# A decoder layer's FFN in three passes: the first pass's down products as seven block products too, an earlier start for the next pass's sums, and other places for the norms' transposes

## Chip, cores and metric

The kernel runs on one core of a Trainium2 chip. The metric is the device time of one execution in microseconds (us), as the median of several runs. TensorE (PE) multiplies, VectorE (DVE) and ScalarE (ACT) work elementwise, GpSimd (POOL) raises a few small tiles to a power, and SyncE (SP) issues the transfers.

## What is computed

One layer of a hybrid decoder on 2048 prompt tokens and 32 sample tokens, in float32 (D = 1024, hidden size 2816, per-layer input of 256):

```
h = h + concat(gated recurrence, conv module) @ w_out        # the mix phase
xn2 = rmsnorm(h, norm_ffn)
h = h + (silu(xn2 @ w_ffn_gate) * (xn2 @ w_ffn_up)) @ w_ffn_down
gate = sigmoid(rmsnorm(h, norm_ple) @ w_ple_gate)
h = h + gate * (p_l @ w_ple_proj)
y = rmsnorm(h, norm_final)
```

## The kernel before

**Arithmetic.** Each float32 operand is split into a high and a low part: ACT copies the rounded high part (L385), DVE subtracts it for the low part (L390, or L393 as a scalar_tensor_tensor where a gain is multiplied in). A product is then three matmuls (high x low, high x high, low x high), which stand in the profile as L542 to L544 for a plain product and as L1627 for one of seven block products. A tile's high part ends in h (wh, xh, x2h, xoh, hxh), its low part in l.

**Phases.** The mix phase goes over 8 blocks of 256 tokens and ends near 960 us. Then the FFN, the per-layer input and the final norm run in three passes t = 0, 1, 2, each over two halves h of 348, 348 and 344 tokens. The hidden size is cut into six chunks of 4, 4, 4, 4, 2 and 4 times 128 (CHUNKS). A pass consists of these stages:

- z, gate and up products (gate_up, L1647): four block products of weights and inputs done as seven by Strassen's sums. The inputs' sums X2[kp] (named A12, A11, S1, S2, S4, S3, A22 for each of four kp) are made by combine(t, kp) (L1371), which norm2(t) starts;
- d, down products of one chunk. In pass 0 they are plain (down, L1827): 8 x 2 x nk products into the residual res, nk the chunk's size. In passes 1 and 2 the chunks of size 4 are made as seven block products for each of four row pairs q (down_sevens, L1750); split_down (L1559) makes the weights' differences, hidden_sums (L1738) the sums of hidden tiles, add_part (L1812) adds each product to the residual. The chunk of size 2 is plain in every pass;
- pin, the per-layer inputs' splits (pin_load, L1969), then p, the embedding stage (embed, L1858): for each of 8 output tiles 16 gate products and 4 projections. norm3 (L1947) splits the residual with its gain for it (h2_split, L1927) and computes the scale row r3; norm4 (L1952) is the final norm with 16 STTs (scalar_tensor_tensor, L393 h<-h,gn,px) and the stores of y.

d of chunks 0 to 3 stands behind the first z of the chunk after; d of chunk 4, d of chunk 5 and p follow one another at the end of a pass.

**A norm's chain** (rms2, L1287): squares and their sums on DVE, a memset (L1310), three transposes of the sums on PE (L1315), two reductions on DVE (L1319, L1322), a power on POOL (L426), three transposes on PE that broadcast the result over all partitions (L1330), and a copy on ACT or the STTs of norm4.

**What sets the order.** The program is written by a list scheduler in Python, Sched (L94). Every piece of work is a generator that asks for buffers of a pool, waits for events and issues instructions. Sched keeps a clock of its own for each engine and records, at every step, the instruction that could start first by these clocks. The order of the records is each engine's order on the chip. An instruction for PE from a side thread (all but lane and ffn) that isn't ready at PE's clock is put back by the number SIDE. The numbers have no meaning on the chip except through the order. Weights come over one DMA queue on SP, into a ring of NRING = 9 pairs of split tiles.

Which chunks take the seven-product form is decided by

```python
def in_sevens(t, c):
    return t in SEVENS and CHUNKS[c] == 4
```

## Time and profile before

| | |
|---|---|
| median of 3 runs | 2650.96 us (2650.74 to 2653.5) |
| profiled execution | 2655.51 us, span 2653.8 us |
| PE busy | 2527.6 us, 95% |
| DVE busy | 1964.1 us, 74% |
| ACT busy | 1070.1 us, 40% |
| mean granted clock of PE | 0.976 |

The span runs from the first to the last instruction in the trace; 1.7 us of the profiled execution lie outside it. "Busy" is the union of an engine's instructions. Matmuls overlap in the trace: one of 348 columns is shown with 0.32 us while the next starts 0.16 us after it, so their spacing is read from starts. The granted clock is 1.00 at TensorE's 2.4 GHz and lower where it ran at 1.2 GHz for part of a stretch.

### The profile page before, as it was taken

What the parts mean: (1) busy time and instruction counts of PE and PEld (TensorE: products, weight loads), DVE (VectorE), ACT (ScalarE), POOL (GpSimd) and SP (SyncE); (2) the same over time, 40 slices, a digit from 0 to 9 for tenths busy, and PEclk for the clock granted to TensorE, in tenths of its full rate; (3) what the DMA queues carried; (4) which work ended last, traced back from release to release, by engine and by line L of the source; (5) the groups of instructions that cost most, each with busy time, mean ns of one, the idle gap of its engine ahead of it and who ended that gap; (6) DMA issues with size and microseconds to landing.
All of it is one profiled execution on the core that took longest, in us unless ns stands there. A gap on an engine that the chain in (4) does not pass through costs nothing.

```text
span 2653.8 us, 44060 instructions
## 1 busy us (share of the span) xinstructions
PE 2527.6 (95%) x15646; PEld 2369.5 (89%) x15646; DVE 1964.1 (74%) x4558; ACT 1070.1 (40%) x2457; POOL 137.9 (5%) x286
## 2 busy tenths in 40 slices
PE   7999999999999799999999799999989799999986
PEld 6987977778888699999999799999989799999976
DVE  8998899678886776676677856786587676667765
ACT  5553344333332343444344343344344233333341
POOL 0111010010110100000000000000000000000000
PEclk9999999999999799999999899999999899999998
DMA  8665745655447674565452475454623645554321
GB/s 312 221 212 186 238 159 191 208 168 168 155 147 207 213 261 155 195 213 179 157 200 72 139 243 182 159 165 168 235 63 104 195 156 191 195 199 164 119 75 51
DMA packets 287630, 465.62 MB, mean 175 GB/s; under 512 B 46256, under 2 KB 87728, under 8 KB 287408
## 3 DMA queue, kind: packets, MB, share of 16 engines
q1 hardware_dynamic: 287408, 462.79, 52.3%
q8 instruction: 123, 2.02, 0.3%
q14 instruction: 99, 0.81, 0.1%
HBM read 363.03 MB, written 99.64 MB: 174 GB/s over the span
## 4 chain that ended last, share of the span: by engine, by line
PE 87%; DVE 6%; DMA 3%; ACT 1%; POOL 1%; issue 1%; SPq 0%; DVEq 0%; ACTq 0%; POOLq 0%
PE pm L1627 27%; PE px L1627 13%; PE pm L542 11%; PE pm L544 11%; PE pm L543 11%; PE px L544 2%; PE px L542 2%; PE px L543 2%; DVE h L390 1%; DVE h L393 1%; PE pm L610 1%; PE pm L612 1%; PE pm L611 1%; DMA wl<-wcl 1%; DVE wl L390 1%; POOL sm L426 1%
## 5 line engine op out<-in xcount | busy, mean ns | idle before, releaser
L390 DVE TENSOR_TENSOR wl<-raw,wh 128x512 fp32r<-128x512 f32 (+1 forms) x476 | 315.2, 666 | 171.4 <-ACT wh L385 167.7
L385 ACT ACTIVATE wh<-raw 128x512 fp32r<-128x512 f32 (+1 forms) x476 | 283.9, 608 | 326.0 <-PE pm L543 112.8
L542 PE MATMUL pm<-xal,wh 128*128 128x256 f32 (+2 forms) x960 | 323.6, 337 | 8.6 <-DVE xal L390 4.5
L544 PE MATMUL pm<-xah,wl 128*128 128x256 f32 (+2 forms) x960 | 310.6, 324 | 1.0 <-DMA wl<-wcl 0.7
L543 PE MATMUL pm<-xah,wh 128*128 128x256 f32 (+2 forms) x960 | 310.4, 323 | 0.0
L542 PE MATMUL pm<-xol,wh 128*128 128x348 f32 (+4 forms) x762 | 254.4, 334 | 6.2 <-DVE h L390 3.6
L544 PE MATMUL pm<-xoh,wl 128*128 128x348 f32 (+4 forms) x762 | 250.0, 328 | 0.6 <-DVE wl L390 0.3
L543 PE MATMUL pm<-xoh,wh 128*128 128x348 f32 (+4 forms) x762 | 249.8, 328 | 0.0
L390 DVE TENSOR_TENSOR h<-pm,h 128x348 f32<-128x348 f32 (+1 forms) x335 | 172.3, 516 | 88.7 <-PE pm L544 42.4
L1627 PE MATMUL pm<-xal,wh 128*128 128x348 f32 (+1 forms) x707 | 228.6, 323 | 3.7 <-DVE f L390 1.8
L1627 PE MATMUL pm<-xah,wh 128*128 128x348 f32 (+1 forms) x707 | 227.8, 322 | 0.0
L1627 PE MATMUL pm<-xah,wl 128*128 128x348 f32 (+1 forms) x707 | 227.5, 322 | 0.1
L542 PEld LDWEIGHTS pm<-xal,wh 128*128 128x128 f32 x960 | 182.8, 190 | 35.7 <-issue 9.2
L393 DVE SCALAR_TENSOR_TENSOR t<-u,cvw,t 128x256 f32<-128x256 f32 x448 | 212.6, 475 | 0.0
L544 PEld LDWEIGHTS pm<-xah,wl 128*128 128x128 f32 x960 | 182.0, 190 | 15.8 <-DMA wl<-wcl 1.8
L543 PEld LDWEIGHTS pm<-xah,wh 128*128 128x128 f32 x960 | 182.7, 190 | 11.7
L385 ACT ACTIVATE wh<-tw 128x512 fp32r<-128x512 f32 x146 | 91.9, 630 | 249.8 <-DVE tw L390 92.9
L1627 PE MATMUL pm<-x2l,wh 128*128 128x348 f32 (+1 forms) x533 | 171.5, 322 | 6.1 <-DVE x2l L390 6.1
L393 DVE SCALAR_TENSOR_TENSOR h<-u,cvw,h 128x256 f32<-128x256 f32 x360 | 170.2, 474 | 2.2 <-ACT h L385 2.1
L1627 PE MATMUL pm<-x2h,wh 128*128 128x348 f32 (+1 forms) x533 | 171.8, 322 | 0.0
L1627 PE MATMUL pm<-x2h,wl 128*128 128x348 f32 (+1 forms) x533 | 171.6, 322 | 0.0
L426 POOL TENSOR_TENSOR sm<-sm,mhalf 128x2 f32<-128x2 f32 (+3 forms) x79 | 72.7, 922 | 1853.9 <-DVE sm L1322 1739.2
(292 smaller groups left out, 6498.4 us busy)
## 6 DMA issues: line engine op xcount, KB each, us to landing
raw<-w_gu SPq DMA_DIRECT2D x220, 256.0 KB, 3.1
wh<-wch SPq DMA_DIRECT2D x192, 256.0 KB, 2.7
wl<-wcl SPq DMA_DIRECT2D x192, 256.0 KB, 3.1
wh<-tch SPq DMA_DIRECT2D x176, 256.0 KB, 4.3
wl<-tcl SPq DMA_DIRECT2D x176, 256.0 KB, 4.6
raw<-w_dn SPq DMA_DIRECT2D x132, 256.0 KB, 3.3
tch<-wh SPq DMA_DIRECT2D x88, 256.0 KB, 2.8
tcl<-wl SPq DMA_DIRECT2D x88, 256.0 KB, 2.9
```

The lines of the kernel that those rows point to most:

```text
L385: nc.scalar.activation(out, in_, func, scale=scale, bias=bias, **kw)
L390: return op("dve", d_tt(n), lambda: nc.vector.tensor_tensor(out=out, in0=a, in1=b, op=o), R, W)
L393: return op("dve", d_tt(n, not isinstance(s, float)), lambda: nc.vector.scalar_tensor_tensor(out=out, in0=a, scalar=s, in1=b, op0=o0, op1= ...
L426: return op("pool", 700.0, lambda: nc.gpsimd.tensor_tensor(out=s.ap[0:rows, out:out + n], in0=s.ap[0:rows, lo:lo + n], in1=mhalf[0:rows, 0 ...
L542: nc.tensor.matmul(out, lhsT=wh, rhs=xl, start=first, stop=False)
L543: nc.tensor.matmul(out, lhsT=wh, rhs=xh, start=False, stop=False)
L544: nc.tensor.matmul(out, lhsT=wl, rhs=xh, start=False, stop=last)
L610: nc.tensor.matmul(bank.ap, lhsT=xs[0], rhs=wl, start=(k == 0), stop=False)
L611: nc.tensor.matmul(bank.ap, lhsT=xs[0], rhs=wh, start=False, stop=False)
L612: nc.tensor.matmul(bank.ap, lhsT=xs[1], rhs=wh, start=False, stop=(k == KD - 1))
L1627: nc.tensor.matmul(out, lhsT=a, rhs=b, start=first and i == 0, stop=last and i == 2, skip_group_check=True)
```

## The change

Three edits. SEVENS takes in pass 0, so its five chunks of size 4 are made as seven block products. SIDE becomes a table by thread name: 4000 for norm, norm_ahead, norm2, norm3 and norm4, 2000 for layer_norm, 1000 for the rest. And norm2(t) for t > 0, before it starts the sums of pass t, no longer waits for the scale rows r3 of pass t - 1; it still waits for the last hidden tiles and for the per-layer inputs' splits.

```diff
-SEVENS = (1, 2)
+SEVENS = (0, 1, 2)
@@
-    SIDE = 1000.0
+    SIDE = dict(norm=4000.0, norm_ahead=4000.0, layer_norm=2000.0, norm2=4000.0, norm3=4000.0, norm4=4000.0)
@@
-                    s += self.SIDE
+                    s += self.SIDE.get(th[0].__name__, 1000.0)
@@
             for k in range(2):
                 for h in HALVES:
                     yield wait(("pin", t - 1, k, h))
-            for h in HALVES:
-                yield wait(("r3", t - 1, h))
```

Two lines fall away, so that lines behind norm2 have numbers lower by two in the changed kernel (L1627 is L1625 there).

What the planner makes of it is seen in the order. First PE at the start of pass 0's embedding stage, from the transposes of the first half's sums (L1315) to the broadcast of their power (L1330). Before:

```order
L544 MATMUL pm_175<-xoh,wl_87 128x348
L1315 MATMUL px_179<-idn,h_77 128x128 x2
L1315 MATMUL px_179<-idn,h_77 92x128
L542 MATMUL pm_175<-xol,wh_86 128x348
L543 MATMUL pm_175<-xoh,wh_86 128x348
L544 MATMUL pm_175<-xoh,wl_87 128x348
...
L542 MATMUL px_181<-hxl,wh_86 128x348
L543 MATMUL px_181<-hxh,wh_86 128x348
L544 MATMUL px_181<-hxh,wl_87 128x348
L1330 MATMUL px_182<-idn,sm_66 128x128 x2
L1330 MATMUL px_182<-idn,sm_66 128x92
```

The dots leave out 12 matmuls. After:

```order
L544 MATMUL px_182<-hxh,wl_87 128x348
L1315 MATMUL px_180<-idn,h_77 128x128 x2
L1315 MATMUL px_180<-idn,h_77 92x128
L542 MATMUL px_182<-xol,wh_86 128x348
L543 MATMUL px_182<-xoh,wh_86 128x348
L544 MATMUL px_182<-xoh,wl_87 128x348
L1330 MATMUL px_179<-idn,sm_66 128x128 x2
L1330 MATMUL px_179<-idn,sm_66 128x92
L542 MATMUL px_182<-hxl,wh_88 128x348
```

Between transposes and broadcast stood 18 matmuls, and now 3.

DVE at the same place: the reductions of the sums (L1319, L1322), then the STT splits of the residual (xol, hxl). Before:

```order
L1319 TENSOR_REDUCE sm_66<-px_179 128x2
L393 SCALAR_TENSOR_TENSOR xol<-h_78,gn,xoh 128x348
L1322 TENSOR_REDUCE sm_66<-px_179 92x1
L393 SCALAR_TENSOR_TENSOR xol<-h_79,gn,xoh 128x348
L393 SCALAR_TENSOR_TENSOR xol<-h_78,gn,xoh 128x348 x2
L390 TENSOR_TENSOR h_78<-pm_177,h_78 128x348
```

After (wl_95, wl_83 and wl_85 are the low parts of the per-layer inputs):

```order
L1319 TENSOR_REDUCE sm_66<-px_180 128x2
L393 SCALAR_TENSOR_TENSOR xol<-h_78,gn,xoh 128x348
L1322 TENSOR_REDUCE sm_66<-px_180 92x1
L393 SCALAR_TENSOR_TENSOR xol<-h_78,gn,xoh 128x348
L393 SCALAR_TENSOR_TENSOR xol<-h_76,gn,xoh 128x348
L393 SCALAR_TENSOR_TENSOR hxl<-h_76,gn,hxh 128x348
L393 SCALAR_TENSOR_TENSOR xol<-h_79,gn,xoh 128x348 x3
L393 SCALAR_TENSOR_TENSOR xol<-h_78,gn,xoh 128x348 x2
L390 TENSOR_TENSOR wl_95<-f_9124,wh_94 128x348
L390 TENSOR_TENSOR wl_83<-h_77,wh_82 128x348
L390 TENSOR_TENSOR wl_85<-h_77,wh_84 128x348
L390 TENSOR_TENSOR h_78<-pm_175,h_78 128x348
```

Behind the second reduction stood 3 STTs before the next addition from PSUM (pm), and now 8 STTs and three splits.

DVE at the head of pass 1, where norm4's 16 STTs of pass 0 (h<-h,gn,px) meet the splits of pass 1's sums (x2l). Before:

```order
L1322 TENSOR_REDUCE sm_71<-px_182 92x1
L393 SCALAR_TENSOR_TENSOR f_9124<-f_9124,gn,r_116 128x348
L393 SCALAR_TENSOR_TENSOR h_77<-h_77,gn,r_116 128x348
...
L393 SCALAR_TENSOR_TENSOR h_76<-h_76,gn,px_179 128x348 x3
L393 SCALAR_TENSOR_TENSOR h_79<-h_79,gn,px_179 128x348 x2
L393 SCALAR_TENSOR_TENSOR h_78<-h_78,gn,px_179 128x348 x3
L393 SCALAR_TENSOR_TENSOR h_76<-h_76,gn,px_182 128x348 x2
L393 SCALAR_TENSOR_TENSOR h_79<-h_79,gn,px_182 128x348 x3
L393 SCALAR_TENSOR_TENSOR h_78<-h_78,gn,px_182 128x348 x3
L390 TENSOR_TENSOR x2l<-f_9127,x2h 128x348
```

After:

```order
L393 SCALAR_TENSOR_TENSOR h_76<-h_76,gn,px_180 128x348 x3
L390 TENSOR_TENSOR wl_87<-raw_103,wh_86 128x512
L393 SCALAR_TENSOR_TENSOR h_79<-h_79,gn,px_180 128x348 x2
L393 SCALAR_TENSOR_TENSOR h_78<-h_78,gn,px_180 128x348 x3
L1322 TENSOR_REDUCE sm_69<-px_179 92x1
...
L390 TENSOR_TENSOR x2l<-f_9125,x2h 128x348
...
L393 SCALAR_TENSOR_TENSOR h_76<-h_76,gn,px_180 128x348 x2
L393 SCALAR_TENSOR_TENSOR h_79<-h_79,gn,px_180 128x348 x3
L393 SCALAR_TENSOR_TENSOR h_78<-h_78,gn,px_180 128x348 x3
L390 TENSOR_TENSOR x2l<-f_9126,x2h 128x348
```

The 16 STTs stood in one row ahead of a split; now they stand in two rows of 8, each behind other splits of sums.

## Rows read from the trace of the kernel before

**Rows 1.** The page's head, its first part (busy time of each engine) and the shares by engine of the chain that ended last.

```profile
span 2653.8 us, 44060 instructions
PE 2527.6 (95%) x15646; PEld 2369.5 (89%) x15646; DVE 1964.1 (74%) x4558; ACT 1070.1 (40%) x2457; POOL 137.9 (5%) x286
PE 87%; DVE 6%; DMA 3%; ACT 1%; POOL 1%; issue 1%; SPq 0%; DVEq 0%; ACTq 0%; POOLq 0%
```

**Rows 2.** What PE waited for over the whole span: the line that waited, the line it waited for, us in total, times, the longest.

```profile
PE px L1330 <- POOL sm L426: 21.3, 9, 5.6
PE px L1315 <- DVE sm L1310: 10.9, 5, 4.5
PE px L1627 <- DVE x2l L390: 9.5, 1, 9.5
```

**Rows 3.** The span in windows: pass 0's z and d stages, pass 0's embedding stage, the head of pass 1, pass 1's embedding stage. Columns: length, busy time (and instructions) of each engine, granted clock of PE, share of the DMA engines, GB/s.

```profile
core 0: us, PE busy (x) PEld busy (x) DVE busy (x) ACT busy (x) POOL busy (x), PEclk, DMA share, GB/s
960.40:1428.60 468.20, 465.14 (x2918) 463.37 (x2917) 320.27 (x574) 205.60 (x395) 2.52 (x2) 1.00 0.53 183
1428.60:1507.00 78.40, 77.88 (x495) 77.53 (x494) 64.37 (x136) 37.28 (x78) 3.27 (x2) 1.00 0.30 97
1507.00:1539.00 32.00, 17.54 (x85) 16.16 (x85) 23.73 (x52) 8.33 (x18) 1.67 (x2) 0.68 0.76 224
1981.00:2072.00 91.00, 82.33 (x497) 80.68 (x498) 72.64 (x154) 44.15 (x93) 6.33 (x2) 0.94 0.31 98
```

**Rows 4.** Timeline of PE at the end of pass 0's embedding stage: the first and the last of 34 matmuls of 348 columns that start one after the other. Columns: start, duration, engine, line, tile.

```profile
1501.75 0.32 PE L542 MATMUL pm<-hxl,wh 128*128 128x348 f32 x1
...
1506.99 0.32 PE L1627 MATMUL px<-xal,wh 128*128 128x348 f32 x1
```

**Rows 5.** Down stages as windows, columns as in rows 3: the first and the last chunk of pass 0 (plain), chunks 0, 1 and 2 of pass 1 (seven products), the last chunk of pass 1 and of pass 2 (seven products).

```profile
1026.10:1058.70 32.60, 32.60 (x204) 32.60 (x205) 17.67 (x31) 5.91 (x10) 0.00 (x0) 1.00 0.32 114
1398.10:1428.60 30.50, 30.50 (x194) 30.50 (x193) 21.96 (x44) 15.84 (x33) 0.00 (x0) 1.00 0.18 56
1592.50:1621.40 28.90, 28.63 (x177) 27.73 (x176) 25.59 (x56) 8.48 (x17) 0.00 (x0) 1.00 0.17 58
1673.90:1702.70 28.80, 28.53 (x175) 27.62 (x175) 25.50 (x56) 8.42 (x17) 0.00 (x0) 1.00 0.17 56
1756.00:1785.40 29.40, 29.01 (x183) 28.23 (x182) 27.95 (x64) 11.63 (x24) 0.85 (x1) 1.00 0.32 105
1951.50:1981.00 29.50, 27.27 (x164) 25.57 (x162) 27.70 (x62) 13.28 (x29) 0.00 (x0) 1.00 0.23 73
2509.40:2538.60 29.20, 26.91 (x165) 25.22 (x163) 27.43 (x62) 13.15 (x29) 0.00 (x0) 1.00 0.23 69
```

**Rows 6.** DVE's instructions by form in pass 1 (1560 to 1950): splits of weights, weight differences and a hidden tile's split (sums and additions of 348 columns take as long). Columns: instructions, busy us, mean ns of one, idle time before them and what ended it.

```profile
L390 DVE TENSOR_TENSOR wl<-tw,wh 128x512 fp32r<-128x512 f32 x35 | 24.2, 691 | 8.2 <-ACT wh L385 7.5
L390 DVE TENSOR_TENSOR tw<-raw,tw 128x256 f32<-128x256 f32 x34 | 14.2, 418 | 0.2
L390 DVE TENSOR_TENSOR xol<-h,xoh 128x348 fp32r<-128x348 f32 x27 | 13.6, 516 | 3.0 <-ACT xoh L385 3.0
L390 DVE TENSOR_TENSOR wl<-raw,wh 128x256 fp32r<-128x256 f32 x17 | 7.1, 415 | 0.0
```

**Rows 7.** Timelines at the start of pass 1's embedding stage: PE from the sums' transposes to where the spacing of matmuls returns to 0.16 us (in brackets idle time before and what ended it), then DVE, then POOL.

```profile
1983.13 0.55 PE L1315 MATMUL px<-idn,h 128*128 128x128 f32 x3
1990.76 0.84 PE L1330 MATMUL px<-idn,sm 128*128 128x128 f32 x3 [5.64 <-POOL sm L426]
1994.20 0.66 PE L542 MATMUL pm<-xol,wh 128*128 128x348 f32 x1 [2.60 <-ACT wh L385]
...
1999.93 0.34 PE L544 MATMUL pm<-xoh,wl 128*128 128x348 f32 x1
...
1985.01 1.55 DVE L393 SCALAR_TENSOR_TENSOR xol<-h,gn,xoh 128x348 fp32r<-128x348 f32 x3
...
1989.43 0.57 DVE L393 SCALAR_TENSOR_TENSOR hxl<-h,gn,hxh 128x348 fp32r<-128x348 f32 x1
...
1985.23 5.48 POOL L426 TENSOR_TENSOR sm<-sm,mhalf 128x3 f32<-128x3 f32 x1 [192.58 <-DVE sm L1322]
```

**Rows 8.** The same at the start of pass 0's embedding stage: PE, DVE, POOL.

```profile
1430.09 0.49 PE L1315 MATMUL px<-idn,h 128*128 128x128 f32 x3
1433.96 0.51 PE L1330 MATMUL px<-idn,sm 128*128 128x128 f32 x3 [0.52 <-POOL sm L426]
...
1431.65 1.55 DVE L393 SCALAR_TENSOR_TENSOR xol<-h,gn,xoh 128x348 fp32r<-128x348 f32 x3
...
1431.81 2.10 POOL L426 TENSOR_TENSOR sm<-sm,mhalf 128x3 f32<-128x3 f32 x1 [218.71 <-DVE sm L1322]
```

**Rows 9.** Timelines at the head of pass 1: PE, then DVE.

```profile
1511.80 1.51 PE L1315 MATMUL px<-idn,f 128*128 128x128 f32 x6 [3.21 <-DVE sm L1310]
1515.01 1.66 PE L1330 MATMUL px<-idn,sm 128*128 128x128 f32 x6 [1.70 <-POOL sm L426]
1526.22 0.66 PE L1627 MATMUL px<-x2l,wh 128*128 128x348 f32 x1 [9.55 <-DVE x2l L390]
...
1532.18 0.40 PE L1627 MATMUL pm<-xah,wl 128*128 128x348 f32 x1
...
1517.85 7.88 DVE L393 SCALAR_TENSOR_TENSOR h<-h,gn,px 128x348 f32<-128x348 f32 x16
```

## The prediction

> **What bounds the kernel now.** I read the page's busy shares first: TensorE (PE) is busy for 95% of the 2653.8 us span, VectorE (DVE) for 74%, and the chain that ended last is 87% PE [rows 1]. So work taken from PE counts nearly in full, as long as nothing else becomes late, and PE's few waits are the other thing to look at. PE's waits [rows 2] name three lines that this change can touch: the broadcast of a norm's scale (L1330, behind POOL's power, 21.3 us over 9 waits), the transposes of a norm's sums (L1315, 10.9 us) and one wait of 9.5 us for a split of a sum of the next pass's inputs (x2l). Third, the stages as windows [rows 3]: the body of pass 0 (960.4 to 1428.6) has PE busy for 465.14 of 468.20 us at full granted clock, and pass 0's embedding stage (to 1507.0) 77.88 of 78.40: nothing to win there but fewer matmuls. The two places where PE stands are the head of pass 1 (1507 to 1539: 17.54 of 32.00 us, clock 0.68) and pass 1's embedding stage (1981 to 2072: 82.33 of 91.00, clock 0.94). The reader should note that the same stage costs 78.4 us in pass 0 and 91.0 us in pass 1, with 495 and 497 matmul records: pass 1 already makes its down products as seven, pass 0 does not.
>
> All my terms are differences against the profiled execution, 2655.51 us (span 2653.8). The runs' median is 2650.96, so I apply the sum to the median. About 0.2% (5.3 us) is what a measurement of this kernel can tell from no change.
>
> **Matmuls removed.** Five of pass 0's six chunks go from 8x2x4 = 64 products to 56, of three matmuls each: 24 less a chunk, 120 in all (PE's order is 120 rows shorter). 34 matmuls start between 1501.75 and 1506.99 [rows 4], 33 steps of 0.1588 us. So 120 x 0.1588 = 19.1 us less PE work. The Trainium skill (TensorE: Matmul & The Clock Gate, Back-to-back issue gap) gives 348/2.4 + 2.5 = 147.5 ns for an isolated matmul, by which the sum would be 17.7, and for a stream of weight loads and matmuls 81 to 131 ns for 128 to 512 columns, which I read as an estimate of some 110 ns, or 13.2 us: a lighter gain. The trace shows neither on these shapes, so 19.1 stays.
>
> **What DVE and ACT get instead.** DVE's order has 250 more TENSOR_TENSORs, 50 a chunk: weight differences (0.418 us), splits of 512 (0.69) and 256 columns (0.415), splits and sums of hidden tiles (0.516), more additions into the residual (0.516) [rows 6]. ACT gets 70 copies; it is busy for 205.6 of 468.2 us in that body [rows 3], so they hide. DVE is the question. In pass 1's seven-product stage 56 instructions take 25.59 us, 0.457 each with their overlap [rows 5]; 250 x 0.457 = 114 us on top of DVE's 320.3 [rows 3] make 434 of the 449 us that PE will need (468.2 - 19.1): 97%. It is hidden only while it lies evenly, and it doesn't: of DVE's order I count 62, 60, 76 and 61 instructions in the first four seven-product stages (30, 30, 40, 30 before), where pass 1 has about 56 to 64.
>
> **First four seven-product stages.** In pass 1 such a stage takes 28.80 to 29.40 us [rows 5], where its 174 to 186 matmuls (three for each product of its order) need 27.6 to 29.5 us at 0.1588; about 1.0 us goes into waiting, with DVE at 0.88 to 0.95. Pass 0's plain stages lose 0.2 us. In pass 0 DVE's work is 62 x 0.457 = 28.3, 27.4, 76 x 0.437 = 33.2 (0.437 being the 27.95 us over 64 of the third window of pass 1) and 27.9 us, against 27.6, 27.6, 29.5 and 27.6 us of PE. The third is 3.7 over; the gate and up products behind it leave DVE room, so part slides past. I give back 4.0 us over the four; the bounds are 0 (all slides) and 9 (each overhang in full, 4.7, and the 1.0 of pass 1 four times).
>
> **The last chunk.** 1398.1 to 1428.6 is PE without a gap, 30.5 us, and would be 26.7 with 168 matmuls; but the same stage takes 29.5 and 29.2 us in passes 1 and 2, DVE 27.70 and 27.43 us busy [rows 5]: 2.8 and 2.5 lost. Pass 0 would have 68 DVE instructions there (62 in pass 1), 30.4 us. I give back 3.5, bounds 2.5 and 5.
>
> **The start of pass 0's embedding stage.** This is the term I hold most against the change. In pass 1 the sums' transposes stand at 1983.13, and 9 matmuls later PE waits 5.64 us for the broadcast at 1990.76: POOL's power (1985.23) takes 5.48 us, while DVE runs an unbroken row of STT splits from 1985.01 to about 1990 [rows 7]. In pass 0 now the power takes 2.10 us, the DVE row is three STTs (1431.65), and 18 matmuls lie between: PE waits 0.52 us [rows 8]. The changed order puts only 3 matmuls between transposes and broadcast in pass 0, and on DVE 8 STT splits and three input splits in a row. Transposes' end to broadcast took 1990.76 - 1983.68 = 7.1 us in pass 1; with 3 matmuls (0.5 us) as cover PE waits 6.6. After such a wait the clock is at its lower level: matmuls start 0.29 us apart until 1999.93 [rows 7]. At the head of pass 1 that lasts from 1526.22 to 1532.18 [rows 9], 6.0 us in which 20 matmuls run that need 3.2, so 2.7 lost. The wait of 2.60 us for a weight's copy on ACT (1994.20) should not return, since ACT's order has this weight's copy ahead of the scale's. So 6.6 + 2.7 = 9.3 less 0.5 of now, say 9.0. Bounds: 2.5 where the power takes 2.10 us as now (1430.58 to 1433.91, less 0.5 cover and the 0.5 of now, no fall of the clock), and 12, the whole of pass 1's excess (91.0 - 497 x 0.1588). The Trainium skill (SBUF — State Buffer, Who interferes with whom) says that a DVE instruction with two SBUF inputs blocks a GpSimd one that reads SBUF; by it the power would end with the row, 8 x 0.49 + 3 x 0.43 = 5.2 us and its own 0.85 later, 0.6 us worse than the row says. The trace agrees in kind: 2.10 us behind three STTs, 5.48 behind ten.
>
> **The head of pass 1.** 32.0 us for 85 matmuls (13.5): 18.5 lost, as waits of 3.21, 1.70 and 9.55 us, the transposes, and 2.7 to the lower clock [rows 9]. The 9.55 is 16 final-norm STTs (7.88 us) ahead of the split that PE needs. The third edit lets the next pass's sums begin earlier, and the new side costs move transposes. In the changed order DVE has the splits of the first sums ahead of these STTs, which stand in two rows of 8; the two transposes stand 12 matmuls apart, and the broadcasts 3 and 18 matmuls after. Walked by hand: about 2.9 us for the first broadcast, 4 for the second (8 STTs 3.9, a weight split 0.6, reduce 0.3 and power 0.85 or more, less 15 matmuls), 3 behind the second 8 STTs, 1.3 of transposes, 2.7 of clock: 14. That is 4.5 better; bounds 0 and 9 (both rows of STTs covered).
>
> **The rest.** The order at the head of pass 2 is nearly as it was (16 STTs still ahead of the sum's split), the mix phase's norms move by some matmuls under waits that total a few us: 0, within 3 either way. The earlier sums and stores use queues that move 183 GB/s in pass 0's body [rows 3], no more bytes.
>
> **Sum.** -19.1 + 4.0 + 3.5 + 9.0 - 4.5 = -7.1, so 2650.96 - 7 = 2644 us.
>
> **Rivals.**
> (1) DVE becomes the bound of pass 0, and it ends slower. Place: the five seven-product stages; for it speak the 97% and the last chunks of passes 1 and 2, which lose 2.8 us at DVE's 0.94; against it the other stages of pass 1, which lose 1.0 at up to 0.95. With 5 us lost in each of the five: -19.1 + 25 + 9 - 4.5 = +10, 2661. It decides against the change from 4 us in each of the first four upward, the other terms as they are. Chance 0.13.
> (2) The seam is mild: pass 0's power finds a gap in the DVE row (2.5), the head of pass 1 gets all 9, the stages give back 2 and 2.5: -19.1 + 4.5 + 2.5 - 9 = -21, 2630. For it: DVE's rows there wait on ACT's copies, and each gap lets POOL in. Against: in pass 1 none did. Chance 0.15.
> (3) Everything is given back: stages 5, last chunk 3.5, embedding 11, head of pass 1 unchanged because its stalls only change names: +0.4, 2651. For it: PE still needs both broadcasts there and DVE's 16 STTs are no fewer. Chance 0.27.
>
> **How the numbers follow.** My forecast, -12 to -2, has 0.45: about 0.33 of it faster, 0.12 within 0.2%. With (2) wholly faster, (3) within but for 0.02, (1) 0.10 slower and 0.03 within: faster 0.50, same 0.40, slower 0.10; I move 0.02 to slower for the mix phase. The range, 2633 to 2655, leaves out half of (2) and most of (1), 0.18.
>
> **What would show it.** PE's order with 120 matmuls less; pass 0's body about 8 to 12 us shorter than 468.2, its seven-product stages at 28.5 to 31 us with waits of PE for DVE; a wait of 5 to 7 us at L1330 (printed with the changed file's line, two less) at the start of pass 0's embedding stage, and that stage at 85 to 90 us instead of 78.4; the head of pass 1 without the single 9.5 us wait. I am wrong if the power there is near 2 us (too pessimistic), if the third stage loses 5 us or more (too optimistic), or if the mix phase moves by more than 3.

## Result: slower, and the profile after

The changed kernel takes 2686.06 us (median of 4 runs, 2685.29 to 2687.66) against 2652.23 us for the kernel before beside it: ratio 1.0121, interval 1.0106 to 1.0136. The forecast of 2644 us and its range to 2655 are both missed, on the side that had a chance of 0.12. Between the profiled executions lie 2685.29 - 2655.51 = 29.8 us, and that is what has to be found.

The page's head, busy times and the chain's shares of the changed kernel, to be read against [rows 1]:

```profile
span 2683.5 us, 44115 instructions
PE 2525.6 (94%) x15526; PEld 2356.6 (88%) x15526; DVE 2058.1 (77%) x4808; ACT 1095.9 (41%) x2527; POOL 147.8 (6%) x286
PE 80%; DVE 10%; DMA 4%; ACT 2%; issue 2%; POOL 2%; SPq 0%; ACTq 0%; DVEq 0%; POOLq 0%
```

120 matmuls are gone, as forecast, but PE's busy time falls by 2.0 us instead of 19.1, since a matmul is shown with 0.32 us or more where the next could start 0.16 us after it (0.40 to 0.66 us behind a wait or at the lower clock, in the rows below), so that short waits vanish under it: in pass 0's body, where PE loses 39 us by the matmuls' starts, 20.6 us stand as gaps. The chain says more: PE's share falls from 87% to 80%, DVE's rises from 6% to 10%. PE's waits over the whole span, against [rows 2]:

```profile
PE px L1330 <- POOL sm L426: 31.0, 7, 7.4
PE pm L1625 <- DVE wl L390: 9.4, 13, 1.3
PE pm L1625 <- ACT wh L385: 8.5, 8, 2.1
```

The waits of these block products for weights' splits (wl, wh) were 0.9 and 0.7 us before. The stages as windows, columns as in [rows 3], to be read against its first three rows: pass 0's z and d stages, its embedding stage, the head of pass 1.

```profile
973.30:1455.60 482.30, 461.68 (x2793) 445.02 (x2791) 406.29 (x809) 224.32 (x450) 1.71 (x2) 0.99 0.51 175
1455.60:1544.30 88.70, 81.61 (x498) 80.98 (x499) 73.40 (x155) 43.97 (x93) 6.70 (x2) 0.94 0.33 107
1544.30:1571.10 26.80, 16.62 (x86) 15.63 (x85) 21.67 (x48) 8.41 (x18) 2.07 (x2) 0.87 0.86 265
```

By their starts and lengths the 29.8 us lie here: the mix phase ends at 973.3 instead of 960.4 (+12.9), pass 0's body takes 482.3 instead of 468.2 (+14.1, though 126 matmuls, 20.0 us, have left this window, so 34 us of waits have come), its embedding stage +10.3 (1.0 us of it six matmuls of the last chunk, which fall into this window now), the head of pass 1 -5.2, pass 1's embedding stage -2.4; pass 2's head gives +1.6 and the end -1.9.

Inside pass 0's body, the first four seven-product stages and the last chunk, columns the same, against [rows 5]:

```profile
1038.20:1068.60 30.40, 29.75 (x176) 27.46 (x175) 27.41 (x62) 9.19 (x19) 0.00 (x0) 1.00 0.20 70
1125.00:1158.40 33.40, 31.73 (x175) 29.13 (x176) 28.99 (x64) 9.24 (x18) 0.00 (x0) 0.95 0.21 73
1214.90:1249.80 34.90, 31.44 (x186) 28.83 (x187) 34.37 (x81) 15.22 (x31) 1.71 (x2) 1.00 0.35 117
1305.00:1337.10 32.10, 30.48 (x174) 27.53 (x175) 29.12 (x65) 9.73 (x19) 0.00 (x0) 1.00 0.22 77
1421.40:1455.60 34.20, 30.14 (x165) 26.98 (x163) 30.50 (x69) 14.84 (x31) 0.00 (x0) 0.95 0.23 74
```

Against the matmuls that start in them (174, 174, 186, 174 and 162) at 0.1588 us they lose 2.8, 5.7, 5.4, 4.5 and 8.5 us. What PE waits for there is seen in the chain that ends at 1160, taken over 1125 to 1160 (the second stage), and, below the dots, the same over 1595 to 1620 of the kernel before, a seven-product stage of pass 1:

```profile
by line: DVE wl L390 21.9%; issue 16.4%; DVE h L390 15.9%; ACT wh L385 12.5%; PE pm L1625 11.3%; PE px L1625 9.1%; DVE tw L390 9.0%; DVE hxl L390 1.5%; DVE f L390 1.4%; ACT h L385 1.3%; ACTq L385 0.4%
...
by line: PE pm L1627 40.9%; PE px L1627 22.9%; DVE wl L390 11.0%; DVE h L390 10.8%; issue 5.6%; ACT wh L385 5.1%; DVE tw L390 4.7%; ACTq L385 0.2%
```

In pass 1 PE carries 64% of the chain. In pass 0 it carries 20%, and the rest goes round between ACT's copy of a weight (wh), DVE's split of it (wl), the weights' differences (tw) and additions into the residual (h). Of that loop, a few steps in order of time (start, duration, engine, tile, line):

```profile
1143.54 0.64 ACT wh L385
1144.20 0.69 DVE wl L390
1144.89 0.43 DVE h L390
1145.32 0.34 DVE tw L390
1145.69 0.44 DVE tw L390
1146.23 0.64 ACT wh L385
...
1150.99 0.64 ACT wh L385
```

From 1143.54 to 1150.99 is one row pair: 7.45 us, where PE needs 6.7 (42 matmuls). ACT stands while DVE makes differences, and DVE stands while ACT copies. What became of DVE's slack is seen in its own waits over the body, before and (below the dots) after:

```profile
DVE wl L390 <- ACT wh L385: 51.0, 65, 1.2
DVE h L390 <- PE pm L544: 42.0, 53, 1.7
DVE h L390 <- PE px L544: 15.3, 27, 1.4
...
DVE wl L390 <- ACT wh L385: 42.1, 72, 1.3
DVE h L390 <- PE pm L1625: 6.4, 16, 0.8
DVE h L390 <- PE px L1625: 2.2, 5, 0.6
```

Before, DVE waited 57 us for these results of PE, which is slack. After, it is 9 us; but some 42 us behind ACT's copies stay. An engine that is 84% busy (406.29 of 482.3) and waits for ACT in another 9% has little left. Whether this is why PE waits is tried below (e13 to e15).

### The profile page after: what moved, and what is told of

It reads as the page before. It is cut to its first block, busy times and chain, and to the rows that moved or that the text cites. A ratio compares the mean times of both kernels' runs of the same rounds, so it can differ in the third digit from the quotient of the medians.

```text
span 2683.5 us, 44115 instructions
## 1 busy us (share of the span) xinstructions
PE 2525.6 (94%) x15526; PEld 2356.6 (88%) x15526; DVE 2058.1 (77%) x4808; ACT 1095.9 (41%) x2527; POOL 147.8 (6%) x286
## 4 chain that ended last, share of the span: by engine, by line
PE 80%; DVE 10%; DMA 4%; ACT 2%; issue 2%; POOL 2%; SPq 0%; ACTq 0%; DVEq 0%; POOLq 0%
PE pm L1625 27%; PE px L1625 13%; PE pm L542 10%; PE pm L544 9%; PE pm L543 9%; DVE h L390 3%; DVE wl L390 2%; PE px L542 1%; PE px L543 1%; PE px L544 1%; POOL sm L426 1%; PE pm L610 1%; DVE h L393 1%; PE pm L612 1%; PE pm L611 1%
## 5 line engine op out<-in xcount | busy, mean ns | idle before, releaser
L390 DVE TENSOR_TENSOR wl<-raw,wh 128x512 fp32r<-128x512 f32 (+1 forms) x476 | 308.0, 654 | 146.4 <-ACT wh L385 137.8
L385 ACT ACTIVATE wh<-raw 128x512 fp32r<-128x512 f32 (+1 forms) x476 | 276.1, 597 | 267.1 <-PE pm L1625 76.0
L385 ACT ACTIVATE wh<-tw 128x512 fp32r<-128x512 f32 x186 | 117.2, 630 | 313.4 <-DVE tw L390 188.7
L390 DVE TENSOR_TENSOR h<-pm,h 128x348 f32<-128x348 f32 (+1 forms) x383 | 196.1, 516 | 52.7 <-PE pm L1625 29.7
L1625 PE MATMUL pm<-xal,wh 128*128 128x348 f32 (+1 forms) x709 | 230.8, 326 | 4.2 <-ACT wh L385 2.1
L1625 PE MATMUL pm<-xah,wl 128*128 128x348 f32 (+1 forms) x709 | 229.2, 323 | 2.1 <-DVE wl L390 2.1
L1625 PE MATMUL pm<-xah,wh 128*128 128x348 f32 (+1 forms) x709 | 229.4, 324 | 0.0
L542 PE MATMUL pm<-xol,wh 128*128 128x256 f32 (+4 forms) x578 | 195.9, 339 | 9.2 <-DVE h L390 5.7
L543 PE MATMUL pm<-xoh,wh 128*128 128x256 f32 (+4 forms) x578 | 191.4, 331 | 0.0
L544 PE MATMUL pm<-xoh,wl 128*128 128x256 f32 (+4 forms) x578 | 191.1, 331 | 0.2
L1625 PE MATMUL pm<-x2l,wh 128*128 128x348 f32 (+1 forms) x531 | 172.4, 325 | 19.2 <-DVE x2l L390 19.2
L426 POOL TENSOR_TENSOR sm<-sm,mhalf 128x2 f32<-128x2 f32 (+3 forms) x79 | 82.2, 1042 | 1884.4 <-DVE sm L1322 1671.4
L1625 PE MATMUL pm<-x2h,wl 128*128 128x348 f32 (+1 forms) x531 | 171.9, 324 | 0.0
L1625 PE MATMUL pm<-x2h,wh 128*128 128x348 f32 (+1 forms) x531 | 171.9, 324 | 0.0
```

Of the source, the lines that this page charges most:

```text
L385: nc.scalar.activation(out, in_, func, scale=scale, bias=bias, **kw)
L390: return op("dve", d_tt(n), lambda: nc.vector.tensor_tensor(out=out, in0=a, in1=b, op=o), R, W)
L426: return op("pool", 700.0, lambda: nc.gpsimd.tensor_tensor(out=s.ap[0:rows, out:out + n], in0=s.ap[0:rows, lo:lo + n], in1=mhalf[0:rows, 0 ...
L542: nc.tensor.matmul(out, lhsT=wh, rhs=xl, start=first, stop=False)
L543: nc.tensor.matmul(out, lhsT=wh, rhs=xh, start=False, stop=False)
L544: nc.tensor.matmul(out, lhsT=wl, rhs=xh, start=False, stop=last)
```

## Experiments

My theories after the result were that the sevens of pass 0 cost the body and its embedding stage, that the SIDE table costs the mix phase, and that the two don't interact; the rivals are in the expectations. For the reading of each run I use stage lengths, taken from the first matmul of a stage to that of the next, in us (z rest: all z stages of a pass but the first; d 0-4: five chunks; head: the first z stage of a pass; 2 p ends 11 us ahead of the span's end):

| kernel | mix end | 0 z rest | 0 d 0-4 | 0 d 5 | 0 p | 1 head | 1 p | 2 head | 2 p |
|---|---|---|---|---|---|---|---|---|---|
| before | 960.4 | 277.4 | 148.9 | 30.5 | 78.3 | 32.1 | 91.2 | 30.4 | 104.2 |
| after | 973.3 | 288.4 | 148.2 | 34.2 | 88.8 | 26.8 | 88.5 | 32.1 | 102.3 |
| e1_sevens | 960.8 | 287.6 | 150.9 | 32.6 | 89.6 | 29.6 | 91.7 | 30.8 | 104.1 |
| e2_side | 975.7 | 277.8 | 148.9 | 30.5 | 78.4 | 33.1 | 89.0 | 34.4 | 104.1 |
| e3_r3 | 959.8 | 277.4 | 148.9 | 30.5 | 78.0 | 12.8 | 91.6 | 30.8 | 105.0 |
| e4_sevens_r3 | 961.3 | 288.2 | 150.2 | 32.6 | 89.4 | 30.6 | 91.5 | 30.4 | 105.0 |
| e5_plain_last | 959.9 | 277.8 | 148.9 | 30.5 | 78.0 | 12.8 | 79.5 | 23.9 | 92.0 |
| e6_first4 | 962.1 | 290.1 | 150.2 | 30.6 | 78.1 | 12.8 | 79.5 | 23.9 | 91.7 |
| e7_first4_inter | 959.0 | 286.7 | 145.1 | 30.6 | 78.1 | 12.8 | 79.4 | 23.9 | 91.8 |
| e8_inter | 964.9 | 287.0 | 142.8 | 34.4 | 85.5 | 30.3 | 84.9 | 31.1 | 97.3 |

Counting the matmuls that start in a stage at 0.1588 us, pass 0's waits went from 4.4 to 12.1 us in the z stages, from 0.7 to 18.6 in d 0-4 and from nothing to 8.5 in d 5.

### Each edit alone

**e1_sevens**: the first edit alone.

```diff
-SEVENS = (1, 2)
+SEVENS = (0, 1, 2)
```

> The kernel before with the first edit alone (pass 0's five wide chunks as seven products; old side cost, old wait for r3). Theory A: in pass 0 the weights' differences and their splits go back and forth between DVE and ACT in DVE's order and set the pace (7.5 us for each q where PE needs 6.7), whatever the other edits do. Then the mix phase is as before (first matmul of pass 0 near 960 us), pass 0's z and d stages take about 482 us as in the changed kernel instead of 468, its embedding stage 87 to 91 instead of 78, and the whole is 18 to 28 us slower than before (2669 to 2679). Rival B: the seven products are slow in pass 0 only because the new side costs and the missing wait put other work among them; then the z and d stages take 455 to 460 us and the whole is 0 to 10 us faster than before.

2681.98 against 2656.15 us, ratio 1.0097 (1.0080 to 1.0113). The body takes 482.6 us, pass 0's embedding stage 89.6, and the mix phase ends where it did. So both losses come from this edit.

**e2_side**: the table SIDE alone (its diff is the second edit's).

> The kernel before with the table of side costs alone. Theory A: the planner's clock of PE is pushed ahead by the side cost, so it believes that a norm's broadcast comes 4 us late and puts weight splits ahead of the norm's work on DVE; the mix phase loses what it lost in the changed kernel: first matmul of pass 0 near 973 instead of 960, and the whole is 8 to 14 us slower than before. Rival B: the mix phase moved for the other two edits (what the planner has to place behind it), and this kernel is within 3 us of before.

2668.72, ratio 1.0046 (1.0030 to 1.0062). The mix phase ends at 975.7, and behind it no stage changes by more than some 4 us. The two parts together, +26 and +13, are some 5 us more than the +34 of the changed kernel's median; about 4 of them lie at the head of pass 1, which takes 26.8 us with all three edits and 29.6 and 33.1 with these alone.

**e3_r3**: the third edit alone.

```diff
-            for h in HALVES:
-                yield wait(("r3", t - 1, h))
```

> The kernel before without the wait of norm2 for r3, and nothing else. The sums of passes 1 and 2 can be made earlier. Theory A (the prediction's): the 16 STTs no longer stand in one row ahead of a split at the head of pass 1 and the stretch from pass 1's first matmul to its second z stage falls from 32 to 24 to 30 us, the whole 2 to 8 us faster. Rival B: the sums move, but PE waits for the same broadcasts and STTs under other names: within 2 us of before.

2639.68, ratio 0.9933 (0.9919 to 0.9948): 16.5 us faster, more than any theory had. The head of pass 1, to be read against the third row of [rows 3]:

```profile
1506.00:1518.80 12.80, 12.80 (x86) 12.72 (x85) 10.55 (x26) 5.30 (x11) 1.70 (x2) 1.00 0.97 346
```

PE has no gap left there. The cause shows in where the first STT of pass 1's sums' inputs stands, before, in e3 and in e4 (next):

```profile
1443.33 0.58 DVE L393 SCALAR_TENSOR_TENSOR h<-h,gn,r 128x348 f32<-128x348 f32 x1
...
1414.42 0.57 DVE L393 SCALAR_TENSOR_TENSOR h<-h,gn,r 128x348 f32<-128x348 f32 x1
...
1460.03 0.57 DVE L393 SCALAR_TENSOR_TENSOR f<-f,gn,r 128x348 f32<-128x348 f32 x1
```

The embedding stage starts at 1428.6 in the first two, at 1443.7 in e4: the sums begin 15 us behind its start, 14 us ahead of it, 16 us behind it.

**e4_sevens_r3**: edits one and three, without the table.

> The changed kernel with the old side cost of 1000 for all (seven products in pass 0, no wait for r3). Theory A: the changed kernel's 34 us fall into some 11 to 14 us of the mix phase, which come back here, and some 20 us of pass 0: 15 to 25 us slower than before, mix phase ending near 960 us. Rival B: the side costs also made pass 0's stages worse; then z and d stages of pass 0 take under 470 us here and the whole is within 8 us of before.

2681.32, ratio 1.0095 (1.0080 to 1.0110), the same as e1: with sevens in pass 0 the third edit is worth nothing. The sums stay late. The traces show one thing that they wait for: norm2 still waits for the splits of the per-layer inputs, whose last ones stand on DVE here in e3 and in e4:

```profile
1409.84 0.51 DVE L390 TENSOR_TENSOR wl<-f,wh 128x348 fp32r<-128x348 f32 x1
...
1452.83 0.95 DVE L390 TENSOR_TENSOR wl<-h,wh 128x348 fp32r<-128x348 f32 x2
```

The first STT follows 4.6 us behind in e3 and 7.2 us in e4. The transfers of these inputs are issued from 1395.5 on in e3 and from 1438.3 on in e4. In the program they are loaded into tiles of a pool (tmp2) that also holds the hidden tiles of a seven-product chunk until their sums are made; that this delays them is likely, but no run tries it alone. e5 and e6 show that it hangs on the last chunk.

### The last chunk

**e5_plain_last**: before, with the third edit, and the last chunk plain in every pass.

```diff
-        return t in SEVENS and CHUNKS[c] == 4
+        return t in SEVENS and CHUNKS[c] == 4 and c != last_chunk
```

> The kernel before without the wait for r3 and with the last chunk of every pass plain (seven products in passes 1 and 2 for chunks 0 to 3 only: 48 matmuls more, 7.6 us). Theory A: the last chunk's seven products save PE 3.8 us, lose 2.8 in the stage itself and put the embedding stage's first broadcast behind a row of DVE work (about 12 us in pass 1) and the next pass's first sums late (about 17 us at the head of pass 2). Then pass 1's embedding stage falls from 91 to about 78 us, the head of pass 2 (its first z stage) from 30 to 13 to 20, pass 2's embedding stage by some us too, and the whole is 2605 to 2620. Rival B: the embedding stage of pass 0 is quick because pass 0 has little DVE work anywhere; then pass 1's stays near 91 us and the whole is 2640 to 2645, slower than without the wait alone by the matmuls.

2613.9 against 2656.13, ratio 0.9847 (0.9830 to 0.9864): 42 us faster than before, the best of all. The chunk's own stage gets 1 us longer (e3 to e5: 29.6 to 30.6 in pass 1), and what follows it shorter by 12 (p, of which 1.0 us is six matmuls of the chunk that now end in their own stage) and 7 (head of pass 2). Pass 1's embedding stage, against the last row of [rows 3]:

```profile
1967.60:2047.00 79.40, 77.96 (x493) 77.54 (x493) 64.03 (x137) 37.83 (x80) 3.70 (x2) 1.00 0.31 95
```

DVE has 137 instructions and 64 us there instead of 154 and 73, and the clock stays at 1.00.

**e6_first4**: e5 with SEVENS = (0, 1, 2), so that pass 0's first four chunks of size 4 alone are new.

> As the kernel with a plain last chunk and no wait for r3, and with seven products for chunks 0 to 3 of pass 0 too (96 matmuls less there, 15.3 us). Theory A: the first four chunks give PE's 15.3 us back in waits for DVE and ACT in the d stages and in the z stages behind them, as in the changed kernel (pass 0's z stages 10 us longer, the first d stages 1 to 2 longer than plain): 8 to 14 us slower than with plain products in pass 0. Rival B: it was the last chunk's end that spoilt pass 0; then this is 5 to 15 us faster than with plain products in pass 0.

2623.7, ratio 0.9883 (0.9863 to 0.9903), 9.8 us slower than e5. The embedding stage and the head of pass 1 stay at 78.1 and 12.8. So their loss belongs to the last chunk, and the body's, less its last chunk, to the first four.

### What makes pass 0's stages slow

**e7_first4_inter** and **e8_inter**: e6 and e4, with split_down making both tiles of differences, X and Y, before it splits either, so that DVE has work while ACT copies.

```diff
         yield less(X, 1, m1, 1, m1, 0)
-        e2 = yield acq(ring)
-        yield from split_piece(X, *e2)
-        w2["s", t, c, q, 1] = e2
-        S.fire(("w2", ("s", t, c, q, 1)))
         Y = yield acq(tw)
         yield less(Y, 0, m1, 1, X, 0)
-        S.release(tw, X)
         yield less(Y, 1, m0, 1, Y, 0)
         S.release(raws, m0)
+        e2 = yield acq(ring)
+        yield from split_piece(X, *e2)
+        S.release(tw, X)
+        w2["s", t, c, q, 1] = e2
+        S.fire(("w2", ("s", t, c, q, 1)))
```

> The same, with the two weight differences of a q made one after the other before either is split, so that DVE needn't wait for ACT's copy between them. The work is the same. Theory A1 (round trips): DVE's path per q falls from 7.5 to about 6.5 us, below PE's 6.7, and the first four chunks' waits go: 8 to 16 us faster than the same without this edit. Theory A2 (load): DVE is simply too full in pass 0, the idle time of 0.3 us per split only moves; within 4 us of the same without this edit.

> The changed kernel with the old side cost (seven products in all five wide chunks of pass 0, no wait for r3) and the two weight differences made before either is split. A1 (round trips): 12 to 20 us faster than without this edit (2661 to 2669). A2 (load): within 4 us of it (2677 to 2685).

e7: 2615.43, ratio 0.9850 (0.9834 to 0.9866), 8.3 us faster than e6, at the lower end of what the theory of round trips had, and no faster than e5. e8: 2662.03, ratio 1.0022 (1.0012 to 1.0033), 19.3 us faster than e4, of which only 6.7 lie in pass 0's body (482.4 to 475.7); the rest are the embedding stages (-3.9, -6.6, -7.7; passes 1 and 2 use split_down too), while the mix phase ends 3.6 us later. The theory of round trips had the gain in pass 0's stages, so its total came out and its place mostly not. The chain of the second stage, e4 and e8 over 1120 to 1160:

```profile
by line: PE pm L1625 27.3%; DVE wl L390 16.1%; DVE h L390 14.0%; issue 13.2%; ACT wh L385 11.7%; PE px L1625 9.6%; DVE tw L390 7.9%; ACTq L385 0.4%
...
by line: PE pm L1625 61.5%; PE px L1625 19.0%; DVE h L390 7.4%; DVE wl L390 5.2%; issue 3.9%; DVE tw L390 3.4%
```

ACT's copies are gone from the chain with the other order alone. The stage's loss, though, falls only from 5.7 to 3.8 us, that of d 0-4 from 20.6 to 14.2, and the last chunk's rises from 6.9 to 8.7: the loop is a part of what PE waits for. The z stages are hardly helped (288.2, 287.0).

**e13_thin_adds**: e4, with pass 0's additions of seven-product results done on 32 of 348 columns (the rest of the residual is left as it was). **e14_thin_adds_inter**: the same on e8. **e15_thin_all**: e13, and pass 0's weight differences on 16 of 128 columns each.

```diff
-        ra = r.ap[:, 0:n]
-        yield tt(ra, bank.ap[:, 0:n], ra, ALU.add, R=[r, bank], W=[r], n=n)
+        w = n if t else 32
+        ra = r.ap[:, 0:w]
+        yield tt(ra, bank.ap[:, 0:w], ra, ALU.add, R=[r, bank], W=[r], n=n)
@@ e15
-            return tt(odd(out, eo), odd(a, ea), odd(b, eb), ALU.subtract, R=[a, b], W=[out], n=256)
+            k = 128 if t else 16
+            return tt(odd(out, eo)[:, :, 0:k], odd(a, ea)[:, :, 0:k], odd(b, eb)[:, :, 0:k], ALU.subtract, R=[a, b],
+                      W=[out], n=256)
```

> The kernel with seven products in all of pass 0 and no wait for r3, where pass 0's additions of the seven products into the residual are made on 32 columns only (so a part of the computation is left out: the residual is not right). Every instruction, its order and its waits stay; 140 additions of 0.43 us (start to start) become about 0.1 us each, some 45 us less DVE work, while the path of the weights (differences on DVE, copy on ACT, low part on DVE) is untouched. Pass 0's z and d stages lose 38 us of their 482 there. If DVE's load is the cause, they fall to 444 to 456. If the round trips of the weights' path set the pace alone, they stay at 465 or more.

> The same with both weight differences of a q made before either is split (a part of the computation is left out as in the one before). With the load gone and fewer round trips in the weights' path pass 0's z and d stages should come down to 444 to 450 us either way; if they stay above 456, something else than DVE makes PE wait (a transfer, or ACT).

> As the kernel with thin additions, and pass 0's weight differences are made on 2 x 16 columns of a tile instead of 2 x 128 (so the down weights of pass 0 are wrong too: a second part of the computation is left out). Order and waits stay; 80 differences of 0.34 us start to start become about 0.1, some 20 us less on DVE and about 1 us less per q in the path of the weights. Thin additions alone left pass 0's z and d stages at 472 us, 28 over PE's own time, in waits at the first products of d stages and of some z stages. Theory A: those products wait for the weights' path, which is one chain through z and d stages (difference, copy, low part, next piece); shorter links let it run ahead: 448 to 460 us. Rival B: they wait for something outside the down weights (the gate and up weights' own differences, a transfer): 466 or more.

2670.63 (ratio 1.0053, 1.0030 to 1.0076), 2654.18 (1.0000, 0.9989 to 1.0011) and 2668.38 (1.0047, 1.0034 to 1.0061). Pass 0's body in e4, e8, e13 and e15 (in e14 it takes 470.7 us):

```profile
961.30:1443.70 482.40, 461.65 (x2792) 445.05 (x2790) 406.15 (x809) 224.31 (x450) 1.71 (x2) 0.99 0.52 175
964.90:1440.60 475.70, 454.04 (x2792) 445.82 (x2790) 408.02 (x814) 224.41 (x455) 1.71 (x2) 0.99 0.54 179
958.50:1430.80 472.30, 457.81 (x2792) 449.88 (x2790) 366.85 (x809) 224.22 (x450) 1.71 (x2) 0.98 0.53 178
960.70:1426.90 466.20, 451.46 (x2793) 445.90 (x2791) 348.77 (x809) 223.99 (x450) 1.71 (x2) 0.99 0.54 181
```

39 us less of DVE work take 10 us from the body, 57 us less take 16, and the other order takes 7; they don't add up (order and thin additions together: 12). Even with DVE at 75% in e15 the body is 23 us above its matmuls (466.2, where 2790 of 0.1588 make 443.1). All three bodies miss what was expected if DVE's load or the down weights' path were the cause (444 to 456, 444 to 450, 448 to 460): e13 lies where its round trips were to leave it, e15 where its rival was. So load counts, but is not all. Nor is DVE's slack what decides: in e15 its waits for PE are back at 48 us (33.6 here and 14.2 for px, where the kernel before had 57), and PE still loses those 23 us:

```profile
DVE h L390 <- PE pm L1627: 33.6, 67, 1.4
```

What is left in e15 stands behind the sums of hidden tiles, here ahead of a z product at 1080:

```profile
1078.88 0.88 ACT L385 ACTIVATE xoh<-f 128x348 fp32r<-128x348 f32 x2 [1.13 <-DVE f L390]
1079.66 1.14 ACT L385 ACTIVATE wh<-raw 128x512 fp32r<-128x512 f32 x2
1080.33 0.43 PE L1627 MATMUL pm<-xal,wh 128*128 128x348 f32 x1 [1.06 <-ACT wh L385]
1081.94 0.42 PE L1627 MATMUL pm<-xah,wl 128*128 128x348 f32 x1 [1.03 <-DVE wl L390]
```

ACT waits 1.13 us for a hidden sum from DVE; behind that copy, in order, stand two weight copies, and PE stands for both in turn.

**e16_ring10**: e4 with one more pair of split tiles, for which two raw tiles are given up.

```diff
-NRING = 9
-NRAW = 6
+NRING = 10
+NRAW = 4
```

> The kernel with seven products in all of pass 0 and no wait for r3, with ten pairs in the ring of split weights instead of nine, and four raw tiles instead of six (SBUF holds no more). Theory A: the ring's look-ahead is what bridges the stretches where DVE is behind; one pair more (0.7 us of DVE work) takes some us off pass 0's z and d stages: 470 to 479 instead of 482. Rival B: the look-ahead is not what limits, or four raw tiles make transfers late: 482 or more.

2672.24, ratio 1.0056 (1.0034 to 1.0079). The body gets longer (489.5 us, z rest 295.7) where 470 to 479 was expected, so this is not the remedy; the whole is about 10 us faster than e4 against its own kernel before, through passes 1 and 2 (p 85.4 and 100.4). Since the edit also took raw tiles, a ring of 10 by itself stays untried.

**e17_sums_later**: e4 with pass 0's hidden sums at a later rank. **e18_first4_later**: the same on e7.

```diff
-                S.spawn(hidden_sums(t, c, j // 2, four), 0)
+                S.spawn(hidden_sums(t, c, j // 2, four), 0 if t else 30)
```

> The kernel with seven products in all of pass 0 and no wait for r3, where pass 0's sums of hidden tiles have a lower rank in the planner (30 instead of 0), so that ACT and DVE take the next weight pieces first; nothing is left out. With additions and down weights thin, pass 0's z and d stages still lost 22 us at the first products behind each burst of hidden sums, where the next stage's first weight copies stand behind the burst in ACT's and DVE's order. Theory A: with the weight pieces ahead these waits go: z and d stages 458 to 472 us instead of 482, the whole 8 to 20 us faster than without this edit. Rival B: the hidden sums are then late for the down products and the waits only change place: 478 or more.

> The kernel with seven products in chunks 0 to 3 of every pass, a plain last chunk, no wait for r3 and both weight differences ahead of the splits (2615 us), with the lower rank for pass 0's sums of hidden tiles. Theory A: pass 0's z and d stages fall below the 449 us that PE needs with plain products there, and the whole is 2598 to 2610, faster than the same with plain products in pass 0 (2614). Rival B: 2612 or more; seven products do not pay in pass 0 at all.

e17: 2664.2, ratio 1.0023 (1.0011 to 1.0035). It is 17 us faster than e4, of which 10 lie in the body (472.2). The z stages' waits fall from 11.9 to 2.5 us, which shows that the hidden sums' place made most of them; but d 0-4 still lose 17.1 (20.6 in e4) and the last chunk 9.5 (6.9), now with

```profile
PE pm L1625 <- DVE xol L390: 7.1, 4, 3.6
```

in the body: splits of the same hidden sums, for which e4 has no wait there. e18: 2616.48, ratio 0.9850 (0.9835 to 0.9864), no faster than e7 or e5, as its rival had it. With the remedies tried here, sevens in pass 0's first four chunks are at best worth nothing.

### What SIDE does to the mix phase

**e9_side_clock**: e2, but the side cost only chooses and is not entered into the planner's clock.

```diff
             th, req = self.ready.pop(i)
+            s = self.start(req)
```

**e12_side_norm** and **e10_side_ffn**: before, with the table's entry for norm alone, and with those of norm2, norm3 and norm4 alone (all others 1000). **e11_best_side**: e5 with the latter.

```diff
@@ e12
+    SIDE = dict(norm=4000.0)
@@ e10 and e11
+    SIDE = dict(norm2=4000.0, norm3=4000.0, norm4=4000.0)
```

> The kernel before with the table of side costs, where the planner uses the side cost only to choose and not for PE's clock and the end of the chosen instruction. Theory A: the mix phase's loss under the new table came from the planner's belief that the first norm's broadcast ends 3 us later than with 1000, by which it put a weight split (whose weights arrive near 19 us) ahead of the norm's first STT on DVE. Then the first norm's STTs start near 15 us again instead of 20.5, the first product near 17 instead of 23, and pass 0 starts 955 to 966 us; the whole is 10 us faster than with the table alone or more. Rival B: it is the choice itself (side work put behind products of the main thread); then pass 0 starts at 970 to 980 as with the table alone.

> The kernel before with a side cost of 4000 for norm alone (the first norm of blocks 0 and 1), 1000 for all others. Theory A: the whole loss of the new table in the mix phase begins here, since the order has the weight split ahead of the first norm's STTs again; the first product comes near 23 us instead of 17, the phase ends 972 to 978 us and the whole is 9 to 15 us slower. Rival B: the later blocks' norms (norm_ahead, layer_norm) make the larger part; then the 6 us of the start are mostly absorbed or stay alone, the phase ends 958 to 968, and the whole is 0 to 7 us slower.

> The kernel before with the new side cost for the FFN's norms alone (norm2, norm3, norm4 at 4000; the mix phase's norms at 1000). Theory A: the mix phase ends near 960 us as before, and the FFN's transposes in other places are worth nothing: within 4 us of before. Rival B: the FFN's new places cost too, 5 us or more slower.

> The kernel without the wait for r3 and with the last chunk plain in every pass, and the new side cost for the FFN's norms. Theory A: within 4 us of the same with 1000 (2614). Rival B: where the last chunk no longer fills DVE, the places matter: 5 us or more off, either way.

e9: 2675.5, ratio 1.0069 (1.0053 to 1.0084), the mix phase ends at 981.1: so the planner's clock wasn't the cause, and the choice itself is left (the rival). e12: 2667.37, ratio 1.0040 (1.0026 to 1.0054), mix end 972.4: the entry for norm alone costs what the table costs. e10: 2657.99, ratio 1.0006 (0.9996 to 1.0015), and e11: 2616.8, ratio 0.9855 (0.9839 to 0.9872): the other places of the FFN's norms are worth nothing, on either base. At the first norm the start looks like this; before, then the changed kernel:

```profile
14.87 1.26 DVE L393 SCALAR_TENSOR_TENSOR t<-h,gn,px 128x256 f32<-128x256 f32 x3
16.52 0.58 PE L542 MATMUL pm<-xal,wh 128*128 128x256 f32 x1 [1.72 <-DVE xal L390]
...
19.37 0.63 ACT L385 ACTIVATE wh<-raw 128x512 fp32r<-128x512 f32 x1 [4.57 <-DMA raw<-w_in]
20.03 0.69 DVE L390 TENSOR_TENSOR wl<-raw,wh 128x512 fp32r<-128x512 f32 x1 [4.17 <-ACT wh L385]
20.64 1.65 DVE L393 SCALAR_TENSOR_TENSOR t<-h,gn,px 128x256 f32<-128x256 f32 x4
22.72 0.58 PE L542 MATMUL pm<-xal,wh 128*128 128x256 f32 x1 [5.32 <-DVE xal L390]
```

A weight's split now stands ahead of the norm's STTs on DVE. Its raw tile comes late (ACT's copy waits 4.57 us for the DMA), so DVE stands for 4.17 us, with the STTs queued behind it, and PE starts 6.2 us later. e12 has the same (its matmul starts at 21.94). That is half of the 12.9 us; the rest comes in later waits (between 200 and 300 us 5.3 us where there were none, and 3 us more between 800 and 990), which no run took apart.

## Why the prediction was wrong

**Matmuls removed** (-19.1): right in number and price. Nothing else in the body came out.

**First four seven-product stages** (+4.0, bounds 0 and 9): the step that failed. They lost 17.9 us more than the plain ones, twice the upper bound. The load itself was over-, not underestimated: the 235 more instructions that fall into the body (of 250) brought 86 us of DVE (320.27 to 406.29), not 114, and DVE ended at 84%, not 97%. What failed is the sentence that it is hidden while it lies evenly: I treated DVE as a stock of time, and took pass 1's 1.0 us a stage at the same busy share as the model. But DVE and ACT take weights from each other one by one and in order. And pass 1 has less of that work: there four of the seven gate and up pieces come ready and split over the DMA queue (170 transfers wh<-tch and wl<-tcl from 1507 to 1981, none in pass 0), while in pass 0 DVE and ACT make and split them as well: 84 differences and 214 splits of 512 columns on DVE in the changed kernel's body, against no difference and 129 splits in pass 1 of the kernel before. Each of order (e8, 7 us), load (e13, 10 us) and the place of the hidden sums (e17, 10 us) gives back a part of the body's 34 us of waits; the parts don't add up (e18 gains nothing on e7), and how the rest divides stays open. That the third stage lost over 5 us (34.9 us for 29.5 of matmuls) is what I had named as showing me wrong.

**The room behind those stages**, into which I let part of the overhang slide, was not there: the z stages lost 7.7 us more, a term that I didn't have. e17 puts most of them on the hidden sums' place.

**The last chunk** (+3.5, bounds 2.5 and 5): 8.4 (7.5 by my count of 168 matmuls; only 162 start in the window). I took passes 1 and 2 as the model here too, and with 168 misread that model: pass 1's stage loses 3.8 us, not 2.8.

**The start of pass 0's embedding stage** (+9.0): right, +10.3 (9.3 without the six matmuls of the last chunk), by the steps named. The lower bound of 2.5 should have been 2.3 by its own numbers. In the changed kernel, PE at transposes and broadcast, then POOL's power, then DVE's first addition from PSUM behind its row:

```profile
1458.57 0.49 PE L1315 MATMUL px<-idn,h 128*128 128x128 f32 x3
1466.40 0.84 PE L1330 MATMUL px<-idn,sm 128*128 128x128 f32 x3 [6.87 <-POOL sm L426]
...
1460.50 5.85 POOL L426 TENSOR_TENSOR sm<-sm,mhalf 128x3 f32<-128x3 f32 x1 [214.25 <-DVE sm L1322]
...
1465.57 0.50 DVE L390 TENSOR_TENSOR h<-pm,h 128x348 f32<-128x348 f32 x1
```

A wait of 6.87 us where 6.6 was forecast, and a power of 5.85 us where pass 1's row had 5.48. It ends at 1466.35, 0.8 us after DVE's row did. By the rule of the Trainium skill (SBUF — State Buffer, Who interferes with whom) the prediction had the power end behind the row, 6.05 us as an estimate; this row lies nearer to it than to pass 1's 5.48, and the trace agrees on when the power gets through. In e6, where the last chunk is plain, the stage is back at 78.1.

**The head of pass 1** (-4.5): -5.2, right in sum, not by the walk. The wait of 9.55 us went, but where I had two waits for broadcasts PE stands three times for splits of sums instead, 10.2 us together, the longest time

```profile
1560.77 0.66 PE L1625 MATMUL pm<-x2l,wh 128*128 128x348 f32 x1 [5.12 <-DVE x2l L390]
```

And I had the worth of the third edit wrong by far: alone it removes 19 us of this head (e3), and the first edit takes that away (e4).

**The rest** (mix phase 0, within 3): the second step that failed, +12.9. I had gone by the waits of before, a few us, and not by the order of DVE, where the split ahead of the first norm's STTs was to be seen.

**The rivals.** Rival 1 came nearest, in place and size: it was priced at 25 us lost in the five stages, and they lost 26 (17.9 and 8.4). That the size fits is in part luck, since its reason, DVE's load at 97%, is not what the runs show: DVE ended at 84%, and with 57 us of its work gone (e15) the body still lost 23 us. What takes its 2661 us further is the z stages and the mix phase, which no rival had. I gave it 0.13 since pass 1 lost only 1.0 us a stage at DVE's 0.95.

**Sum.** -19.1 for the matmuls, + 7.7 + 17.9 + 8.4 for the body's waits, + 12.9 for the mix phase, + 9.3 - 5.2 and -2.7 for what follows the body make +29.2, against 29.8 measured.

## To carry to other kernels

Work that is moved to an engine which serves the bound one has to be priced along the order of that engine and of its partner, round trip by round trip: 84% busy did not leave 16% to spend here. That the idle time which ended with the bound engine had gone (57 us before, 9 after) was a warning, but its return is no all-clear: in e15 it was back at 48 us, and PE still waited behind the order of the pieces. A cheaper form of the last stage ahead of a seam can cost more behind the seam than it saves: in pass 1 seven products in the last chunk take 1 us from their stage and add 12 to the next and 7 to the next pass's head. And an edit's worth can hang on another: the earlier start of sums gave 16.5 us alone and nothing beside the first edit, so edits that come together are to be priced together and tried apart.

## What the runs showed of the hardware

An addition on 32 columns is not a tenth of one on 348: in e13, grouped by form over pass 0's body,

```profile
L390 DVE TENSOR_TENSOR h<-pm,h 128x32 f32<-128x32 f32 x96 | 18.0, 188 | 19.7 <-PE pm L1625 18.9
```

it takes 0.188 us where 348 columns take 0.516 in the same run. By these two a column costs 1.04 ns and an instruction 0.155 us besides.
